# Attention gates and attention branch, four units between the groups of the state-space mixer

## The chip, the cores and the metric

The kernel runs on one core of one Trainium2 chip. The metric is device time of one execution in microseconds (us). TensorE (PE in the rows) multiplies, VectorE (DVE), ScalarE (ACT) and GpSimd (POOL) do elementwise work, and the queue of SyncE (SP) issues most loads from DRAM.

## The reference

A model of two blocks on a sequence of 256 tokens with 1024 features, each block in two layers. The change is in the first block, whose layer reads

```python
u = rms_norm(h, norm_mix[layer])
z, xbc, dt_raw, q, k, v, g_ssd, g_attn = jnp.split(u @ w_in[layer], IN_SPLITS, axis=-1)
y_ssd = ssd_mixer(z, xbc, dt_raw, ...)      # causal conv, SSD in 4 groups of 8 heads, norm per group
y_attn = dilated_attention_mixer(q, k, v, cos, sin)
merged = (jax.nn.sigmoid(g_ssd) * (y_ssd @ w_ssd_branch[layer])
          + jax.nn.sigmoid(g_attn) * (y_attn @ w_attn_branch[layer]))
h = h + merged @ w_out[layer]
u = rms_norm(h, norm_ffn[layer])
h = h + (jax.nn.silu(gate) * up) @ w_down[layer]
```

In `ssd_mixer` the 2048 channels of `x` go through a convolution over 4 tokens and a silu; per group a decay matrix is multiplied into `C B^T` and then with `x * dt`; the result is gated by `silu(z)` and normed over the group's 512 channels. All in float32.

## The kernel before

Every weight matrix is cut into units of 128 x 1024 numbers. `plan()` lists the units in the order of their use, and the weights lie in DRAM in that order, two units to one load of 1 MB (`raw`, three buffers). Each unit is split into a high part `wh` (ScalarE cast, L151) and a low part `wl` = raw - wh (L154, on VectorE or GpSimd), three buffers each, at most `LEAD` = 2 units ahead of the one in use. A product of float32 is then three matmuls: high by high (L465), high by low (L466) and low by high (L467, the one that needs `wl`). A unit of kind "A" has 8 slices of the contraction, so 24 matmuls of 128x256, and adds to a PSUM bank `mm` (three banks); two units (`pairA`) fill a bank.

While `pool_every` = 4 is set (from B and C to the last gate of the state-space mixer), each unit whose number in the plan is divisible by 4 has its low part made by GpSimd (`wl` on POOL), the others by VectorE.

In a layer of the first block come: V, K and Q with attention's two halves, B and C, and then 56 units that concern the change. I number them 0 to 55 in each kernel's own order. Before, they are four groups of eight (four XS units with convolution and silu, four Z units with silu), then eight units of the attention gate (GA), eight of the attention branch, eight of the gate of the state-space mixer (GS). In layer 0 GpSimd's low parts fall on units 0, 4, 8, ..., in layer 1 on units 2, 6, 10, ...; the change leaves this so. After them comes `w_ssd_branch`, in which each output takes two units of 1024 rows: the first reads groups 0 and 1 of the mixer (`yh`, `yl`), the second groups 2 and 3.

Work beside the weights is written as generators. After every unit `tick()` takes one step of each queue: `qa` (attention), `qs` (`ssd_group`) and `qt` (`ssd_tail`). `ssd_group` has six steps: C B^T and its mask `cb` (VectorE, L643), `xdt`, and for each of four pairs of heads the decay `M`: a minimum on VectorE (L659, reads the broadcast `abc`), six exponentials on ScalarE (L668), the product with `cb` on GpSimd (L669), two steps later the matmuls (L678, L679), and then `xs` (L684, L686). The tail squares (`sq`, GpSimd L696 and L697), takes the inverse root (L351, L352), broadcasts it by matmuls (`ch<-c,gr`, L710), scales `xs` (L714) and splits it into `yh` (ScalarE, L359) and `yl` (VectorE, L390).

The order of the program is a wish only: a scheduler lays out each engine's queue before the run, and it may move an instruction ahead of others when its inputs come earlier. On the chip each engine then takes its queue strictly in order. `M` has three buffers, `abc`, `cb` and `xdt` one each; `xs` and `sz` two.

Of the kernel before, what the change touches and what calls it, by code (L numbers as in the profile page):

```python
# [10 lines left out]
F32 = mybir.dt.float32  # L11
F32R = mybir.dt.float32r
BF16 = mybir.dt.bfloat16
AF = mybir.ActivationFunctionType
ALU = mybir.AluOpType
# [3 lines left out]
P = 128  # L19
S = 256  # L20
D = 1024
# [8 lines left out]
C_Z, C_XS, C_B, C_C, C_DT, C_Q, C_K, C_V, C_GS, C_GA = (  # L30
    0, 2048, 4096, 4608, 5120, 5152, 8224, 9248, 10272, 11296)
# [20 lines left out]
def plan():  # L52

    u = []

    def slab(name, layer, k, c0, kind="B", order=None):
        for r in order or range(k // 256):
            u.append((kind, name, layer, 256 * r, c0))  # L60

    def col(name, layer, c0, k=1024):
        for r in range(0, k, 1024):
            u.append(("A", name, layer, r, c0))

    for l in range(DEPTH):
        for n in range(2):
            slab("w_ple_2", l, 256, 512 * n)
    for l in range(DEPTH):
        for half in range(2):  # L70
            slab("w_in", l, D, C_V + 512 * half)
            for c in (C_K, C_Q, C_Q + 1024, C_Q + 2048):
                for f in range(4):
                    col("w_in", l, c + 512 * half + 128 * f)
        for f in range(8):
            col("w_in", l, C_B + 128 * f)
        for g in range(4):
            for f in range(4):
                col("w_in", l, C_XS + 512 * g + 128 * f)
            for f in range(4):  # L80
                col("w_in", l, C_Z + 512 * g + 128 * f)
        for f in range(8):
            col("w_in", l, C_GA + 128 * f)
        for f in range(8):
            col("w_attn_branch", l, 128 * f)
        for f in range(8):
            col("w_in", l, C_GS + 128 * f)
        for f in range(8):
            col("w_ssd_branch", l, 128 * f, 2048)
        for n in range(2):  # L90
            slab("w_out", l, D, 512 * n)
        slab("w_gate_up", l, D, 0, "C")
        for p in range(1, NPAIR):
            for j in (0, 128):
                col("w_gate_up", l, 256 * p + j)
            for j in (0, 128):
                col("w_gate_up", l, FFN + 256 * p + j)
        for n in range(2):
            slab("w_down", l, FFN, 512 * n)
    for l in range(DEPTH):  # L100
        for s in (4, 5, 6):
            slab("w_in_2", l, D, 512 * s)
        for f in range(8):
            col("w_in_2", l, 128 * f)
        for s in (2, 7, 3):
            slab("w_in_2", l, D, 512 * s)
        for n in range(2):
            slab("w_out_2", l, D, 512 * n, order=OUT2_ORDER)
        for n in range(2):
            slab("w_ple_gate_2", l, D, 512 * n)  # L110
    return u


class Weights:


    def __init__(self, tc, nc, dram, raw_pool, hl_pool):
        self.tc = tc
        self.nc, self.dram, self.raw_pool, self.hl_pool = nc, dram, raw_pool, hl_pool
        self.plan = plan()  # L120
        self.end = len(self.plan)
        self.raw = {}
        self.hl = {}
        self.dma_at = self.split_at = self.at = 0
        self.own = {}
        self.first = -9
        self.pool_every = 0
# [130 lines left out]
class Net:  # L258
# [459 lines left out]
    def block1(self, l, h, u, uh, ul):  # L718
        nc = self.nc
# [4 lines left out]
        qa, qs, qt = [], [], []  # L724
# [7 lines left out]
        os = [self.pair([P, 4, S], "O0", "O1")]  # L732
# [9 lines left out]
        for f in range(0, 8, 2):  # L742
            ps = self.pairA("w_in", l, C_B + 128 * f, D, getu)
            self.conv_pair(l, ps, 16 + f, bc[:, f:f + 2, :])
            if f == 0:
                self.drain(qa)
                os.append(self.pair([P, 4, S], "A0", "A1"))
                qa.append(self.attention(*B, *os[1]))
        ytags = ["A2", "A3", "A4", "B0", "B1", "B2", "B3", "B4"]
        ys = []  # L750
        for g in range(4):
            xs = self.sp.tile([P, 4, S], F32, tag="xs", name="xs", bufs=2)
            sz = self.sp.tile([P, 4, S], F32, tag="sz", name="sz", bufs=2)
            for f in (0, 2):
                ps = self.pairA("w_in", l, C_XS + 512 * g + 128 * f, D, getu)
                self.conv_pair(l, ps, 4 * g + f, xs[:, f:f + 2, :])
            for f in (0, 2):
                ps = self.pairA("w_in", l, C_Z + 512 * g + 128 * f, D, getu)
# [4 lines left out]
            yh, yl = self.pair([P, 4, S], ytags[2 * g], ytags[2 * g + 1])  # L763
            ys.append((yh, yl))
            qs.append(self.ssd_group(l, g, bc, xs, sz, dts, yh, yl, qt))

        def halves(tiles):
            return [tiles[f // 4][:, f % 4:f % 4 + 2, :] for f in range(0, 8, 2)]

        ga = halves([self.sp.tile([P, 4, S], F32, tag="u", name="ga", bufs=2) for _ in range(2)])  # L770
        for f in range(0, 8, 2):
            ps = self.pairA("w_in", l, C_GA + 128 * f, D, getu)
            nc.scalar.activation(ga[f // 2], ps, AF.Tanh, scale=0.5)
        self.drain(qa)
        for f in range(0, 8, 2):
            ps = self.pairA("w_attn_branch", l, 128 * f, D, lambda k: (*os[k // 4], k % 4))
            nc.vector.scalar_tensor_tensor(ga[f // 2], ga[f // 2], 1.0, ps, ALU.add, ALU.mult)
        gs = self.sp.tile([P, KD, S], F32, tag="big", name="gs")
        for f in range(0, 8, 2):
            ps = self.pairA("w_in", l, C_GS + 128 * f, D, getu)  # L780
# [4 lines left out]
        for f in range(0, 8, 2):  # L785
# [3 lines left out]
            ps = self.pairA("w_ssd_branch", l, 128 * f, 2 * D, lambda k: (*ys[k // 4], k % 4))  # L789
# [30 lines left out]
        for p in range(1, NPAIR):  # L820
# [10 lines left out]
            f = 2 * (p % 2)  # L831
# [372 lines left out]
def _layout(x):  # L1204
    w = np.empty((len(plan()), P, 1024), np.float32)
    for n, (kind, name, l, r, c) in enumerate(plan()):
        k, width = (8, 128) if kind == "A" else (2, 512)
        m = x[name][l, r:r + k * P]
        if kind == "A" and name == "w_in" and C_Q <= c < C_V:
            m = m[:, c + ROPE1]  # L1210
            c = 0
        m = m[:, c:c + width] if kind != "C" else np.concatenate([m[:, c:c + 256], m[:, FFN + c:FFN + c + 256]], axis=1)
        w[n] = m.reshape(k, P, width).transpose(1, 0, 2).reshape(P, 1024)
    w = np.ascontiguousarray(w.reshape(-1, 2, P, 1024).transpose(0, 2, 1, 3)).reshape(-1, P, 2048)
    wdt = x["w_in"][:, :, C_DT:C_DT + 32].reshape(DEPTH, 8, P, 32).transpose(2, 0, 1, 3).reshape(P, DEPTH, 256)
    conv = np.concatenate([x["conv_w"], x["conv_b"][:, None, :]], axis=1)
    conv = conv.reshape(DEPTH, 5, 24, P).transpose(3, 0, 2, 1).reshape(P, DEPTH, 120)
    dsk = np.repeat(x["d_skip"], 64, axis=1).reshape(DEPTH, 16, P).transpose(2, 0, 1)
    sn = x["ssd_norm"].reshape(DEPTH, 16, P).transpose(2, 0, 1)
    feat = np.concatenate([conv, dsk, sn], axis=2)  # L1220
    rows = np.stack([x["dt_bias"][0], x["a_log"][0], x["dt_bias"][1], x["a_log"][1]])
    i, j = _positions()
    bias2 = np.take(x["rel_bias_2"], _bucket(np.maximum(i - j, 0)), axis=0).transpose(0, 2, 1)
    pT = x["p_2"][:, 0].transpose(0, 2, 1).reshape(DEPTH, 2, P, S).transpose(0, 2, 1, 3)
    c1, c2 = _consts()
    out = dict(w=w, wdt=wdt, feat=feat, rows=rows, bias2=bias2, pT=pT, consts=c1, consts2=c2, x=x["x"][0])
    for n in ("norm_mix", "norm_ffn", "norm_final", "norm_g_2", "ret_norm_g_2", "q_norm_g_2", "k_norm_g_2",
              "ple_norm_g_2"):
        out[n] = x[n]
    return {n: np.ascontiguousarray(v) for n, v in out.items()}  # L1230
# [19 lines left out]
```

## Time and profile before

| | |
|---|---|
| median of 3 runs | 1624.92 us (1623.88 to 1625.94) |
| the profiled execution | 1624.88 us |
| its span of instructions | 1623.1 us |
| TensorE busy in the span | 1569.8 us |
| VectorE, ScalarE, GpSimd busy | 1126.9, 800.7, 485.2 us |
| data from HBM | 278.69 MB, mean 174 GB/s |

The profiled execution's time is its span and 1.8 us around it. In layer 0 the 56 units run from about 180 to 384 us of the span, in layer 1 from about 810 to 1025 us. A matmul counts as busy until its modelled end, so TensorE's busy share says little on its speed; its idle time and the number of instructions in a stretch (the figure behind x) say more.

### The profile page before, as it was taken

To read this page: it belongs to the slowest core of one execution; us is meant where nothing else is said; L and a number is where in the kernel's file an instruction comes from. 1 tells how busy PE (TensorE), PEld (TensorE's weight loads), DVE (VectorE), ACT (ScalarE), POOL (GpSimd) and SP (SyncE) were. 2 spreads that over 40 slices of the span, in tenths; PEclk is the share of its full clock that TensorE was granted. 3 is DMA by queue.
4 is the path that set the end of the run, shared out by engine and by line. 5 is a ranking of instruction groups with operands and counts; after the bars stand their busy time and mean duration, and the time that the engine had idled before them with its cause. 6 is when DMAs were issued, how large, how long until landed. Compare 5 with 4: busy or idle time off the path is not lost.

```text
span 1623.1 us, 26819 instructions
## 1 busy us (share of the span) xinstructions
PE 1569.8 (97%) x10904; PEld 1443.0 (89%) x10904; DVE 1126.9 (69%) x1634; ACT 800.7 (49%) x1256; POOL 485.2 (30%) x298
## 2 busy tenths in 40 slices
PE   9999999999999999999999889999999899989998
PEld 6999989899989987899998889988998679868986
DVE  5768998964665655677899865465565667666765
ACT  5444667544434444344476654443443445454543
POOL 3546257731020001245445753010000252141212
PEclk9999999999999999999999999999999999999999
DMA  8544534465545555454444445554555555454542
GB/s 348 172 167 143 191 136 156 165 215 183 182 168 183 182 184 205 156 180 158 150 164 134 178 141 202 185 205 143 183 184 193 192 190 188 144 181 147 185 149 104
DMA packets 43373, 284.67 MB, mean 175 GB/s; under 512 B 4817, under 2 KB 6225, under 8 KB 10866
## 3 DMA queue, kind: packets, MB, share of 16 engines
q1 hardware_dynamic: 41314, 271.37, 48.5%
q0 software_dynamic: 1936, 11.60, 1.8%
q8 instruction: 85, 1.39, 0.3%
q14 instruction: 38, 0.31, 0.1%
HBM read 278.69 MB, written 4.26 MB: 174 GB/s over the span
## 4 chain that ended last, share of the span: by engine, by line
PE 84%; DVE 7%; POOL 3%; ACT 3%; issue 2%; DMA 1%; SPq 0%; POOLq 0%; ACTq 0%; DVEq 0%
PE mm L465 17%; PE mm L467 17%; PE mm L466 17%; PE mm L402 8%; PE mm L403 8%; PE mm L404 8%; PE tr L366 2%; DVE u L210 2%; DVE wl L154 2%; DMA raw<-in_w_dram 1%; PE ch L523 1%; POOL wfirst L154 1%; ACT wh L151 1%; PE ch L678 1%; ACT wfirst L151 1%
## 5 line engine op out<-in xcount | busy, mean ns | idle before, releaser
L154 DVE TENSOR_TENSOR wl<-raw,wh 128x1024 fp32r<-128x1024 f32 x422 | 573.7, 1364 | 310.5 <-ACT wh L151 308.9
L151 ACT CAST wh<-raw 128x1024 fp32r<-128x1024 f32 x454 | 474.3, 1048 | 560.2 <-PE mm L466 395.5
L467 PE MATMUL mm<-uh,wl 128*128 128x256 f32 x2176 | 617.9, 284 | 9.3 <-DVE wl L154 5.9
L465 PE MATMUL mm<-uh,wh 128*128 128x256 f32 x2176 | 620.5, 285 | 1.6 <-ACT wh L151 1.1
L466 PE MATMUL mm<-ul,wh 128*128 128x256 f32 x2176 | 616.2, 283 | 0.0
L467 PEld LDWEIGHTS mm<-uh,wl 128*128 128x128 f32 x2176 | 411.6, 189 | 11.5 <-DVE wl L154 6.6
L465 PEld LDWEIGHTS mm<-uh,wh 128*128 128x128 f32 x2176 | 411.8, 189 | 6.3 <-issue 4.2
L466 PEld LDWEIGHTS mm<-ul,wh 128*128 128x128 f32 x2176 | 411.4, 189 | 1.3 <-issue 0.9
L154 POOL TENSOR_TENSOR wfirst<-raw,wfirst 128x1024 fp32r<-128x1024 f32 x24 | 62.0, 2594 | 550.9 <-ACT wfirst L151 550.7
L154 POOL TENSOR_TENSOR wl<-raw,wh 128x1024 fp32r<-128x1024 f32 x32 | 77.2, 2412 | 108.7 <-ACT wh L151 98.8
L403 PE MATMUL mm<-wl,uh 128*128 128x512 f32 (+1 forms) x220 | 87.2, 396 | 0.4 <-DVE wl L154 0.3
L404 PE MATMUL mm<-wh,ul 128*128 128x512 f32 (+1 forms) x220 | 86.2, 392 | 0.0
L402 PE MATMUL mm<-wh,uh 128*128 128x512 f32 (+1 forms) x220 | 86.0, 400 | 0.0
L485 POOL TENSOR_TENSOR qT<-qT,rot 64x512 f32<-64x512 f32 x32 | 57.4, 1794 | 92.8 <-ACT qT L481 92.8
L669 POOL TENSOR_TENSOR M<-M,cb 128x768 f32<-128x768 f32 x32 | 67.9, 2138 | 12.9 <-DVE cb L643 6.5
L629 DVE SCALAR_TENSOR_TENSOR acc<-mm,feat,acc 128x255 f32<-128x255 f32 (+2 forms) x144 | 67.2, 475 | 5.2 <-ACT acc L627 4.1
L402 PE MATMUL mm<-wfirst,uh 128*128 128x512 f32 (+1 forms) x140 | 58.3, 416 | 2.2 <-ACT uh L382 1.2
L403 PE MATMUL mm<-wfirst,uh 128*128 128x512 f32 (+1 forms) x140 | 57.4, 410 | 0.3 <-DVE wfirst L154 0.3
L404 PE MATMUL mm<-wfirst,ul 128*128 128x512 f32 (+1 forms) x140 | 56.6, 404 | 0.0
L486 POOL TENSOR_TENSOR qT<-qT,rp 64x512 f32<-64x512 f32 x32 | 49.8, 1555 | 20.7 <-DVE rp L483 20.7
L465 PE MATMUL mm<-A,wh 128*128 128x256 f32 x192 | 54.0, 281 | 0.0
L466 PE MATMUL mm<-B,wh 128*128 128x256 f32 x192 | 54.0, 281 | 0.0
(298 smaller groups left out, 2695.9 us busy)
## 6 DMA issues: line engine op xcount, KB each, us to landing
raw<-in_w_dram SPq DMA_DIRECT2D x243, 1024.0 KB, 4.8
abc<-scr POOLq DMA_DIRECT2D x8, 1024.0 KB, 6.1
es<-e POOLq DMA_DIRECT2D x4, 512.0 KB, 11.4
e<-es SPq DMA_DIRECT2D x4, 512.0 KB, 5.0
raw<-in_w_dram SPq DMA_DIRECT2D x2, 512.0 KB, 5.0
h<-in_x_dram SPq DMA_DIRECT2D x2, 512.0 KB, 8.9
h<-in_x_dram SPq DMA_DIRECT2D x1, 1024.0 KB, 5.7
gain<-in_norm_ffn_dram SPq DMA_DIRECT2D x2, 512.0 KB, 5.3
```

The source lines that it names most:

```text
L151: self.nc.scalar.copy(h, raw)
L154: eng.tensor_tensor(lo, raw, h.bitcast(F32), ALU.subtract)
L402: nc.tensor.matmul(ps, xh[:, k0 + k, ts], hw[:, k, :], start=start and k == 0, stop=False)
L403: nc.tensor.matmul(ps, xh[:, k0 + k, ts], lw[:, k, :], start=False, stop=False)
L404: nc.tensor.matmul(ps, xl[:, k0 + k, ts], hw[:, k, :], start=False, stop=stop and k == 1)
L465: nc.tensor.matmul(ps, hw[:, k, :], xh[:, kx, :], start=j == 0 and k == 0, stop=False)
L466: nc.tensor.matmul(ps, hw[:, k, :], xl[:, kx, :], start=False, stop=False)
L467: nc.tensor.matmul(ps, lw[:, k, :], xh[:, kx, :], start=False, stop=j == n - 1 and k == 7)
L485: nc.gpsimd.tensor_tensor(dst[0:64], dst[0:64], self.cc1[0:64, None, :].to_broadcast([64, 2, S]), ALU.mult)
L486: nc.gpsimd.tensor_tensor(dst[0:64], dst[0:64], b[0:64], ALU.add)
L629: nc.vector.scalar_tensor_tensor(acc[:, j, k:S], ps[:, j, 0:S - k], w[:, 3 - k:4 - k], acc[:, j, k:S], ALU.mult, ALU.add)
L669: nc.gpsimd.tensor_tensor(m, m, cb[:, None, :].to_broadcast([P, 2, 384]), ALU.mult)
```

## The change

The list of units and the body of `block1` change in the same way. After group 0 and after group 1 come four units of the attention gate each, after group 2 and after group 3 four units of the attention branch each. GS follows as before. So the 56 units are now: group 0 in 0 to 7, gate 8 to 11, group 1 in 12 to 19, gate 20 to 23, group 2 in 24 to 31, branch 32 to 35, group 3 in 36 to 43, branch 44 to 47, GS 48 to 55. The number of instructions stays, `drain(qa)` ahead of the branch goes (the one in group 1 remains), and the tiles of the gate are taken ahead of the loop. The line numbers of the changed kernel are one higher in the helpers and 14 higher in the Z part of the loop.

```diff
@@ plan()
-        for f in range(8):
-            col("w_in", l, C_GA + 128 * f)
-        for f in range(8):
-            col("w_attn_branch", l, 128 * f)
+            for f in range(4 * (g % 2), 4 * (g % 2) + 4):
+                if g < 2:
+                    col("w_in", l, C_GA + 128 * f)
+                else:
+                    col("w_attn_branch", l, 128 * f)
@@ block1()
+        ga = halves([self.sp.tile([P, 4, S], F32, tag="u", name="ga", bufs=2) for _ in range(2)])
+
+        def gate(f):
+            ps = self.pairA("w_in", l, C_GA + 128 * f, D, getu)
+            nc.scalar.activation(ga[f // 2], ps, AF.Tanh, scale=0.5)
+
+        def branch(f):
+            ps = self.pairA("w_attn_branch", l, 128 * f, D, lambda k: (*os[k // 4], k % 4))
+            nc.vector.scalar_tensor_tensor(ga[f // 2], ga[f // 2], 1.0, ps, ALU.add, ALU.mult)
+
         for g in range(4):
...
             qs.append(self.ssd_group(l, g, bc, xs, sz, dts, yh, yl, qt))
-        ga = halves([self.sp.tile([P, 4, S], F32, tag="u", name="ga", bufs=2) for _ in range(2)])
-        for f in range(0, 8, 2):
-            ps = self.pairA("w_in", l, C_GA + 128 * f, D, getu)
-            nc.scalar.activation(ga[f // 2], ps, AF.Tanh, scale=0.5)
-        self.drain(qa)
-        for f in range(0, 8, 2):
-            ps = self.pairA("w_attn_branch", l, 128 * f, D, lambda k: (*os[k // 4], k % 4))
-            nc.vector.scalar_tensor_tensor(ga[f // 2], ga[f // 2], 1.0, ps, ALU.add, ALU.mult)
+            for f in (4 * (g % 2), 4 * (g % 2) + 2):
+                (gate if g < 2 else branch)(f)
```

Three places show what moved. First VectorE in layer 1 while group 0 is worked off beside the last head of attention (`acc`, `xs<-xs,acc`: convolution and silu; `M`, `xs<-xs,feat,ch`: `ssd_group`; `E,m`: attention). Before:

```order
L154 TENSOR_TENSOR wl<-raw,wh 128x1024
L629 SCALAR_TENSOR_TENSOR acc<-mm,feat,acc 128x255
L629 SCALAR_TENSOR_TENSOR acc<-mm,feat,acc 128x254
L629 SCALAR_TENSOR_TENSOR acc<-mm,feat,acc 128x253
L659 TENSOR_TENSOR M<-abc,d_acum 128x2x2x128
L154 TENSOR_TENSOR wl<-raw,wh 128x1024
L659 TENSOR_TENSOR M<-abc,d_acum 128x2x2x128
L629 SCALAR_TENSOR_TENSOR acc<-mm,feat,acc 128x255
L629 SCALAR_TENSOR_TENSOR acc<-mm,feat,acc 128x254
L629 SCALAR_TENSOR_TENSOR acc<-mm,feat,acc 128x253
L684 SCALAR_TENSOR_TENSOR xs<-xs,feat,ch 128x256 x2
L629 SCALAR_TENSOR_TENSOR acc<-mm,feat,acc 128x255
```

and now:

```order
L155 TENSOR_TENSOR wl<-raw,wh 128x1024
L660 TENSOR_TENSOR M<-abc,d_acum 128x2x2x128
L155 TENSOR_TENSOR wl<-raw,wh 128x1024
L660 TENSOR_TENSOR M<-abc,d_acum 128x2x2x128
L685 SCALAR_TENSOR_TENSOR xs<-xs,feat,ch 128x256 x2
L526 ISA E,m_9115<-ch,mask_a 128x256
L526 ISA m_9115 128x1
L528 ISA E,m_9115<-ch,mask_a 128x128
L528 ISA m_9115 128x1
```

The convolution of group 1 no longer stands among these rows; it comes later in the queue.

Second GpSimd's queue in layer 0 from the tail of group 0 over the start of `ssd_group` 1 (`E`: attention, `M`: decay, `sq` and `gr`: tail, `abc`: broadcast of the next group). Before:

```order
L686 TENSOR_TENSOR xs<-xs,sz 128x512
L541 TENSOR_TENSOR E<-E 128x384
L696 TENSOR_TENSOR sq<-sq 128x512
L669 TENSOR_TENSOR M<-M,cb 128x768 x2
L697 TENSOR_TENSOR sq<-sq 128x256
L669 TENSOR_TENSOR M<-M,cb 128x768
L154 TENSOR_TENSOR wl<-raw,wh 128x1024
L352 TENSOR_TENSOR gr<-rs_v,nhalf 128x2
```

and now:

```order
L687 TENSOR_TENSOR xs<-xs,sz 128x512
L542 TENSOR_TENSOR E<-E 128x384
L697 TENSOR_TENSOR sq<-sq 128x512
L698 TENSOR_TENSOR sq<-sq 128x256
L353 TENSOR_TENSOR gr<-rs_v,nhalf 128x2
L155 TENSOR_TENSOR wl<-raw,wh 128x1024
L670 TENSOR_TENSOR M<-M,cb 128x768 x3
L155 TENSOR_TENSOR wl<-raw,wh 128x1024
L639 DMA abc<-scr 128x2048
```

The squares of the tail stand ahead of the three products `M` and no longer among them, and a low part `wl` now stands directly behind the three.

Third VectorE in layer 1 at the end of the 56 units (`rs_v`, `xs<-xs,feat,ch`, `B`: tail of group 3; `ga`, `gs`: gates). Before:

```order
L351 TENSOR_SCALAR rs_v<-ch 128x2
L154 TENSOR_TENSOR wl<-raw,wh 128x1024 x2
L777 SCALAR_TENSOR_TENSOR ga<-ga,mm 128x512
L714 SCALAR_TENSOR_TENSOR xs<-xs,feat,ch 128x256 x4
L390 TENSOR_TENSOR B_10009<-xs,B_10008 128x1024
L154 TENSOR_TENSOR wl<-raw,wh 128x1024
L777 SCALAR_TENSOR_TENSOR ga<-ga,mm 128x512
L154 TENSOR_TENSOR wl<-raw,wh 128x1024 x2
L777 SCALAR_TENSOR_TENSOR ga<-ga,mm 128x512
L154 TENSOR_TENSOR wl<-raw,wh 128x1024 x10
L791 SCALAR_TENSOR_TENSOR gs<-gs,mm 128x512
```

and now:

```order
L685 SCALAR_TENSOR_TENSOR xs<-xs,feat,ch 128x256 x2
L155 TENSOR_TENSOR wl<-raw,wh 128x1024 x3
L352 TENSOR_SCALAR rs_v<-ch 128x2
L155 TENSOR_TENSOR wl<-raw,wh 128x1024 x2
L715 SCALAR_TENSOR_TENSOR xs<-xs,feat,ch 128x256 x4
L155 TENSOR_TENSOR wl<-raw,wh 128x1024
L391 TENSOR_TENSOR B_10387<-xs,B_10386 128x1024
L155 TENSOR_TENSOR wl<-raw,wh 128x1024 x3
L795 SCALAR_TENSOR_TENSOR gs<-gs,mm 128x512
```

The scaling and the split of the last group's `xs` have moved behind the low parts of GS, to directly ahead of `gs`, which belongs to `w_ssd_branch`.

## Rows read from the trace of the kernel before

**Rows 1.** Busy time by engine, whole span: us, share, instructions.
```profile
PE 1569.8 (97%) x10904; PEld 1443.0 (89%) x10904; DVE 1126.9 (69%) x1634; ACT 800.7 (49%) x1256; POOL 485.2 (30%) x298
```

**Rows 2.** Stretches of 20 us: busy us by engine, granted clock, DMA.
```profile
220.00:240.00 20.00, 17.82 (x143) 15.83 (x142) 19.02 (x38) 10.66 (x23) 10.40 (x7) 1.00 0.45 151
240.00:260.00 20.00, 19.11 (x151) 17.81 (x151) 16.69 (x23) 15.75 (x35) 16.57 (x11) 1.00 0.34 113
...
280.00:300.00 20.00, 19.69 (x163) 17.57 (x161) 19.96 (x26) 10.31 (x18) 16.22 (x10) 1.00 0.54 200
300.00:320.00 20.00, 18.95 (x158) 18.43 (x155) 19.12 (x21) 15.11 (x31) 14.57 (x7) 1.00 0.38 125
320.00:340.00 20.00, 19.68 (x166) 18.07 (x166) 15.53 (x17) 10.91 (x18) 12.47 (x9) 1.00 0.63 218
...
400.00:420.00 20.00, 20.00 (x171) 20.00 (x170) 11.52 (x13) 8.60 (x9) 0.00 (x0) 1.00 0.56 184
...
860.00:880.00 20.00, 16.28 (x135) 15.32 (x134) 19.93 (x34) 12.25 (x26) 10.96 (x8) 1.00 0.32 108
...
900.00:920.00 20.00, 15.56 (x122) 14.52 (x119) 19.66 (x22) 13.33 (x28) 15.15 (x7) 0.96 0.31 107
...
940.00:960.00 20.00, 14.76 (x106) 14.27 (x105) 13.42 (x11) 8.52 (x16) 12.06 (x6) 0.83 0.32 106
```

**Rows 3.** Stretches of 5 us in layer 1, same columns.
```profile
920.00:925.00 5.00, 5.00 (x38) 4.68 (x37) 3.08 (x8) 1.95 (x4) 1.39 (x2) 0.80 0.57 203
955.00:960.00 5.00, 4.74 (x24) 4.74 (x25) 0.20 (x1) 0.06 (x1) 0.79 (x1) 0.55 0.62 210
960.00:965.00 5.00, 5.00 (x45) 4.57 (x44) 1.99 (x3) 2.90 (x5) 1.55 (x2) 1.00 0.35 100
```

**Rows 4.** Waits of PE, layer 1, 840 to 960 us: total, times, longest.
```profile
PE mm L467 <- DVE wl L154: 4.9, 1, 4.9
PE mm L467 <- POOL wl L154: 2.9, 1, 2.9
PE tr L366 <- DVE E L543: 2.0, 1, 2.0
```

**Rows 5.** Waits of PE, layer 0, 200 to 345 us, same columns.
```profile
PE tr L366 <- DVE E L543: 2.2, 1, 2.2
```

**Rows 6.** DVE in order of time: start, duration, instruction, idle before it.
```profile
308.79 0.55 DVE L643 TENSOR_TENSOR cb<-ch,c 128x384 f32<-128x384 f32 x1
...
936.69 0.68 DVE L632 SCALAR_TENSOR_TENSOR xs<-xs,acc 128x512 f32<-128x512 f32 x1
...
951.83 3.38 DVE L154 TENSOR_TENSOR wl<-raw,wh 128x1024 fp32r<-128x1024 f32 x1
961.02 1.23 DVE L154 TENSOR_TENSOR wl<-raw,wh 128x1024 fp32r<-128x1024 f32 x1 [5.81 <-ACT wh L151]
...
991.38 1.65 DVE L714 SCALAR_TENSOR_TENSOR xs<-xs,feat,ch 128x256 f32<-128x256 f32 x4
```

**Rows 7.** POOL in order of time, layer 0, then layer 1.
```profile
309.51 6.87 POOL L669 TENSOR_TENSOR M<-M,cb 128x768 f32<-128x768 f32 x3 [2.73 <-DVE cb L643]
316.35 2.27 POOL L696 TENSOR_TENSOR sq<-sq 128x512 f32<-128x512 f32 x1
318.58 2.39 POOL L154 TENSOR_TENSOR wl<-raw,wh 128x1024 fp32r<-128x1024 f32 x1
...
951.79 2.33 POOL L154 TENSOR_TENSOR wl<-raw,wh 128x1024 fp32r<-128x1024 f32 x1
```

**Rows 8.** PE in order of time, layer 0, then layer 1.
```profile
305.94 0.59 PE L640 MATMUL ch<-bc 128*128 128x256 f32 x2
...
309.43 0.60 PE L366 MATMUL tr<-c,xs 128*128 128x128 f32 x4
...
990.58 0.61 PE L710 MATMUL ch<-c,gr 128*128 128x128 f32 x4
```

**Rows 9.** ACT in order of time, layer 1.
```profile
993.07 1.05 ACT L359 CAST B<-xs 128x1024 fp32r<-128x1024 f32 x1 [1.35 <-DVE xs L714]
```

More of the change, by code (lines that the diff above doesn't have):

```diff
@@ L748, in block1, with halves @@
                 qa.append(self.attention(*B, *os[1]))
+        def halves(tiles):
+            return [tiles[f // 4][:, f % 4:f % 4 + 2, :] for f in range(0, 8, 2)]
+        ga = halves([self.sp.tile([P, 4, S], F32, tag="u", name="ga", bufs=2) for _ in range(2)])
[5 more added lines that the diff above has]
+            nc.vector.scalar_tensor_tensor(ga[f // 2], ga[f // 2], 1.0, ps, ALU.add, ALU.mult)
         ytags = ["A2", "A3", "A4", "B0", "B1", "B2", "B3", "B4"]
@@ L765, in block1 @@
             qs.append(self.ssd_group(l, g, bc, xs, sz, dts, yh, yl, qt))
-        def halves(tiles):
-            return [tiles[f // 4][:, f % 4:f % 4 + 2, :] for f in range(0, 8, 2)]
-        ga = halves([self.sp.tile([P, 4, S], F32, tag="u", name="ga", bufs=2) for _ in range(2)])
-        for f in range(0, 8, 2):
-            ps = self.pairA("w_in", l, C_GA + 128 * f, D, getu)
-            nc.scalar.activation(ga[f // 2], ps, AF.Tanh, scale=0.5)
-        self.drain(qa)
-        for f in range(0, 8, 2):
-            ps = self.pairA("w_attn_branch", l, 128 * f, D, lambda k: (*os[k // 4], k % 4))
-            nc.vector.scalar_tensor_tensor(ga[f // 2], ga[f // 2], 1.0, ps, ALU.add, ALU.mult)
+            for f in (4 * (g % 2), 4 * (g % 2) + 2):
+                (gate if g < 2 else branch)(f)
         gs = self.sp.tile([P, KD, S], F32, tag="big", name="gs")
```

## The prediction

> **What bounds the kernel now.** I read the busy times first: TensorE is busy for 1569.8 us of a span of 1623.1 us [rows 1], so an order that changes no work can win only from the 53 us in which it is idle and from stretches in which its clock falls. Next I cut the span into stretches of 20 us and looked for those in which TensorE is short of 20.00. In the 56 units of layer 0 it is short by 2.18 us in 220 to 240, 0.89 in 240 to 260, 0.31, 1.05 and 0.32 in the three from 280 to 340: 4.75 us [rows 2]. In layer 1 it is 3.72 us in 860 to 880, 4.44 in 900 to 920 and 5.24 in 940 to 960: 13.4 us [rows 2]. The reader is to see VectorE in the same rows: 19.02, 19.96, 19.12, 19.93 and 19.66 of 20 us where TensorE starves, against 11.52 us in 400 to 420, where nothing but units and their low parts run and TensorE does 171 instructions without a gap [rows 2]. So work of VectorE is heaped on the groups, and the gate and branch units behind them have slack.
>
> The idle time in layer 1 also costs clock. In 920 to 925 and 955 to 960 the granted clock is 0.80 and 0.55, each behind a wait, and TensorE does 38 and 24 instructions where a stretch at 1.00 holds 45 [rows 3]. That is 7/45 of 5 us = 0.8 us, and 4.74 us less 24/9 us = 2.0 us: 2.8 us. All that the groups lose is thus 4.75 + 13.4 + 2.8 = 21.0 us.
>
> Third, the waits by name. The two longest in layer 1 are for low parts `wl`, 4.9 us for one of VectorE and 2.9 us for one of GpSimd [rows 4]; after them, in both layers, TensorE's transpose waits for attention's `E`, 2.0 and 2.2 us [rows 4, 5]. The queues show why low parts come late. A VectorE low part takes 1.23 us alone (at 961.02) and 3.38 us beside a low part of GpSimd that began 0.04 us before it and took 2.33 us [rows 6, 7]; so what GpSimd does delays VectorE as well. And GpSimd works its three products `M` in one go once `cb` is there, 6.87 us, then `sq` 2.27 us, then `wl` 2.39 us: the low part is done 11.5 us after the burst began [rows 7].
>
> The Trainium skill states this as a rule (SBUF — State Buffer, "Who interferes with whom"): a VectorE instruction with two SBUF inputs and a GpSimd instruction that reads SBUF cannot run at once, and the later one waits out the other. By that rule the low part at 951.83 should take 2.33 + 1.23 = 3.56 us, and the row has 3.38, so the trace agrees.
>
> **What the change does, part by part.** Nothing is added or removed: the same units, low parts, loads and steps. What moves are 16 units a layer, at 24 matmuls each. TensorE's 171 instructions in 20 us [rows 2] make 2.8 us for a unit, so each group gets four units, 11.2 us, in which VectorE has little but low parts. A group's own work runs in the six ticks after it, so four of its six steps now fall into those units.
>
> Gain, layer 0. The wait for `E` of 2.2 us stands in the first ticks behind group 0, where TensorE's queue and GpSimd's are as before; I keep it. The others, 4.75 - 2.2 = 2.6 us, go. Layer 1: the same kind of wait, 2.0 us, I keep, since `E` is behind GpSimd work there too; the other 11.4 us go, and with them the 2.8 us of clock, since no wait of 3 us or more is left. Sum of the gain: 2.6 + 11.4 + 2.8 = 16.8 us. Its bounds: 21.0 us if the waits for `E` go too, and nothing if the waits only move.
>
> Cost, the low part behind the burst. In layer 0 GpSimd's queue has a `wl` directly behind the three `M` of groups 1, 2 and 3, and TensorE wants it at units 24, 36 and 48. I count from the broadcast of the tail, which comes about when the unit four places earlier starts. VectorE and GpSimd: broadcast 0.61 [rows 8], scaling 1.65, a low part 1.23, the silus of Z and XS 0.68 each, the tail's low part 1.23 (the form of a `wl`), `cb` 0.55 [rows 6], then the three `M` 6.87 and `wl` 2.39 [rows 7]: 15.9 us. TensorE: broadcast 0.61, four units 11.2, C B^T 0.59, two sets of transposes at 0.60 [rows 8], and about as much again for the first products of the pairs: 14.2 us. So it waits 1.7 us, three times: 5.1 us. The bounds are 0 (VectorE takes some of these rows before the broadcast) and 4.0 us each (`M` and `wl` as far apart as before, with 2.27 us between them).
>
> In layer 1 the low part behind the burst follows only after the next broadcast's load, the fourth `M` and an `xs`, and is wanted two units later. The same sequence stood there before, five units behind `cb`, and TensorE's waits have only one for a GpSimd low part, 2.9 us, which came behind a burst and `sq` [rows 4]. So each of the three costs between 0 and 2.9 us; the nearest row is the sequence that cost nothing, and I take 0.5 us each: 1.5 us.
>
> Cost, the last tail. It had 12 units of cover and now ends with GS. Its chain is 0.61 + 1.65 + 1.05 for the cast [rows 6, 8, 9] and 1.23 for the low part, 4.5 us; one low part of a unit stands between scaling and split on VectorE, mostly beside the cast: 4.7 us. `w_ssd_branch` needs group 3 in the middle of its second unit, 0.61 + 1.5 x 2.8 = 4.8 us on. I take 0.2 us a layer, 0.4 us; if a cast and a low part get ahead it is 1.05 + 1.23 = 2.3 us a layer.
>
> What costs nothing: the tiles of the gate are taken earlier, from buffers that the norm's `u` left before; the load of `h` for the residual goes out five loads later on SP's queue, behind the last use of `abc`, and its reader comes only with `w_out`, 16 units on. Were that cover gone, the loads of two or three units would stand behind it. PSUM banks for the new units are those of the old ones.
>
> Sum: 16.8 - 5.1 - 1.5 - 0.4 = 9.8 us less. The profiled execution took 1624.88 us, its span and 1.8 us; the median is 1624.92. So 1624.9 - 9.8 = **1615.1 us**.
>
> **Rivals.** (1) All waits go: if VectorE has slack in every stretch, `cb` and `E` come early too. 1624.9 - 21.0 = 1603.9 us. For it speaks the load: VectorE had 19 to 20 of 20 us busy and gets a third more time for each group. Against it: both waits for `E` sit beside GpSimd's work, which stays.
>
> (2) The waits move with the bursts. GpSimd's seconds are the same, each group still has its burst behind `cb`, and VectorE's low parts beside it take 3.38 instead of 1.23 us. If each burst holds TensorE for 2.5 to 3 us, six of them give back 15 to 18 us of the 16.8: 1623 to 1626 us. For it: both long waits of layer 1 lie beside such bursts. Against it: `sq` has left the burst, and VectorE has less queued behind it. The skill's rule above is this rival's: issue order, not load, decides who waits, so thinner load on VectorE would not help.
>
> (3) Slower: the low part behind the burst, in both layers. If `cb` is as late as the rows add up and the burst runs with the 2.27 us more that it had, TensorE waits 4.0 us at units 24, 36 and 48 of layer 0 and 26, 38 and 50 of layer 1: 24 us, against a gain of 16.8. 1624.9 - 16.8 + 24 = 1632 us. It decides from 2.8 us a wait on. Against it: layer 1 has two units, 5.6 us, more than layer 0.
>
> (4) The last tail is late: 2.3 us twice on top of the forecast instead of 0.4: 1615.1 + 4.2 = 1619.3 us.
>
> **How the numbers follow.** Forecast 0.46 (its own range 1609 to 1620), rival 1 0.16, rival 2 0.19, rival 3 0.10, rival 4 0.09. About 0.2% or 3.2 us is what a measurement of this kernel can tell from no change. Faster is then the forecast, rivals 1 and 4 and a little of 2: 0.73. The same is most of rival 2: 0.17. Slower is rival 3: 0.10. The range from 1605 to 1622 us leaves out most of rivals 2 and 3 above and the fastest end of rival 1 below; its ends take in 0 to 2.5 us for each wait of layer 0.
>
> **What would show it.** Right: in layer 1 VectorE's busy time in the stretches from 860 to 960 falls below 19 us, the waits of 4.9 and 2.9 us are gone, no stretch there has a clock under 0.9, and both layers take about equally long for the 56 units; small waits for a `wl` of GpSimd appear at units 24, 36 and 48 of layer 0. Rival 2 would show six waits of 2.5 us beside `M`, rival 3 waits of 4 us, rival 4 a wait of TensorE in the second unit of `w_ssd_branch`. Wrong altogether would be a wait at a place that none of these names.

## The result, and the profile after

The changed kernel takes 1606.65 us (median of 4 runs, 1604.33 to 1611.75) against 1625.43 us for the kernel before on the same chip (4 runs, 1623.88 to 1626.95): a ratio of 0.9889, 95% interval 0.9863 to 0.9915. It is faster by 18.8 us (by the interval 14 to 22), where 9.8 were forecast. Its profiled execution took 1607.53 us, 1605.7 of them the span.

First the page's busy times [rows 1]:

```profile
PE 1567.0 (98%) x10904; PEld 1440.6 (90%) x10904; DVE 1118.2 (70%) x1634; ACT 801.5 (50%) x1256; POOL 490.2 (31%) x298
```

TensorE's work is the same 10904 matmuls; its idle time in the span fell from 53.3 to 38.7 us. To see where, I cut out the 56 units of each layer, from the first matmul of unit 0 to that of the unit behind unit 55 (columns: stretch, its length, busy us of PE, PEld, DVE, ACT and POOL, granted clock, DMA share, GB/s). Before, layer 0 and layer 1:

```profile
179.80:383.50 203.70, 198.94 (x1627) 189.47 (x1626) 164.87 (x262) 124.49 (x226) 109.78 (x63) 1.00 0.51 175
810.00:1025.20 215.20, 201.63 (x1618) 191.51 (x1617) 166.50 (x250) 124.21 (x225) 109.16 (x61) 0.98 0.48 167
```

After:

```profile
177.70:383.20 205.50, 201.74 (x1627) 191.24 (x1625) 164.92 (x258) 124.61 (x226) 113.91 (x63) 0.99 0.50 173
809.80:1007.60 197.80, 196.96 (x1619) 188.12 (x1617) 152.50 (x245) 123.35 (x225) 109.88 (x61) 1.00 0.52 182
```

Layer 1 gained 17.4 us, 12.7 of it TensorE's idle time (13.57 to 0.84); layer 0 lost 1.8. Layer 0 began 2.1 us earlier; 17.4 - 1.8 + 2.1 is the span's 17.4 within 0.3. Those 2.1 us come from the start of the kernel, which the change leaves alone. From 20 to 40 us, before and after:

```profile
20.00:40.00 20.00, 18.09 (x87) 14.63 (x86) 8.63 (x12) 8.77 (x15) 9.67 (x8) 0.91 0.94 389
20.00:40.00 20.00, 18.95 (x104) 15.79 (x104) 9.56 (x13) 9.94 (x16) 9.67 (x8) 1.00 0.95 393
```

The profile before has 0.9 us more of waits of TensorE there, a granted clock of 0.91 and 17 matmuls fewer. The new order with place 2 (below) has 0.91 and 87 matmuls there too, so this is not the order's doing. The part that the two profiles show of the order itself is 17.4 - 1.8 = 15.6 us.

The stretches of 20 us that answer to [rows 2], one of layer 0 and three of layer 1, and one stretch of 5 us in layer 0:

```profile
220.00:240.00 20.00, 19.13 (x140) 17.39 (x141) 13.65 (x27) 11.16 (x27) 10.19 (x7) 0.91 0.44 158
...
860.00:880.00 20.00, 20.00 (x171) 19.41 (x169) 18.24 (x33) 16.43 (x36) 9.23 (x7) 1.00 0.37 113
...
900.00:920.00 20.00, 19.16 (x161) 18.10 (x160) 14.00 (x19) 14.20 (x30) 12.91 (x8) 1.00 0.52 189
...
940.00:960.00 20.00, 20.00 (x168) 18.60 (x167) 13.33 (x23) 15.29 (x33) 12.98 (x9) 1.00 0.54 186
...
220.00:225.00 5.00, 4.13 (x20) 3.61 (x21) 3.65 (x5) 2.34 (x7) 0.64 (x1) 0.70 0.43 123
```

In layer 1 the clock is 1.00 and TensorE is full but for the 0.84 us in 900 to 920, which is the wait for `sq` below. VectorE goes from 19.93, 19.66 and 13.42 us to 18.24, 14.00 and 13.33: in the stretch in which TensorE had lost most, 940 to 960, its load is as it was. In layer 0 the granted clock is 0.70 of 2.4 GHz in the stretch that holds a wait, so TensorE ran a part of it at 1.2 GHz.

TensorE's waits (total, times, longest; one of 0.2 us left out) in layer 0 from 175 to 400 us [rows 5]:

```profile
PE tr L367 <- DVE E L544: 2.2, 1, 2.2
PE ch L703 <- POOL sq L698: 1.0, 1, 1.0
PE mm L468 <- POOL wl L155: 0.2, 1, 0.2
```

and the only one in layer 1, from 790 to 1060 us [rows 4]:

```profile
PE ch L703 <- POOL sq L698: 0.8, 1, 0.8
```

The waits of 4.9 and 2.9 us for low parts are gone, and so is layer 1's wait for `E`. GpSimd's queue shows what changed (start, duration, instruction, idle before it). Layer 1 before, ahead of the low part at 951.79 of [rows 7]:

```profile
943.73 5.90 POOL L669 TENSOR_TENSOR M<-M,cb 128x768 f32<-128x768 f32 x3 [3.81 <-DVE cb L643]
949.59 2.24 POOL L696 TENSOR_TENSOR sq<-sq 128x512 f32<-128x512 f32 x1
```

Layer 1 after, group 1:

```profile
884.49 2.40 POOL L155 TENSOR_TENSOR wl<-raw,wh 128x1024 fp32r<-128x1024 f32 x1 [2.53 <-ACT wh L152]
888.33 8.29 POOL L670 TENSOR_TENSOR M<-M,cb 128x768 f32<-128x768 f32 x3 [1.44 <-DVE cb L644]
...
902.79 2.38 POOL L155 TENSOR_TENSOR wl<-raw,wh 128x1024 fp32r<-128x1024 f32 x1
```

Before, the low part stood behind the three `M` and half of `sq`, and the low part of VectorE for which TensorE waited 4.9 us ran beside it (951.83, 3.38 us). Now one is made ahead of the burst and the next only 6 us after its end. The order of the units did not change which units GpSimd serves; it changed what stands in front of them.

### The profile page after: what moved, and what is told of

Same layout as the page of the kernel before. It is cut to its first block, busy times and chain, and to the rows that moved or that the text cites. A ratio compares the mean times of both kernels' runs of the same rounds, so it can differ in the third digit from the quotient of the medians.

```text
span 1605.7 us, 26834 instructions
## 1 busy us (share of the span) xinstructions
PE 1567.0 (98%) x10904; PEld 1440.6 (90%) x10904; DVE 1118.2 (70%) x1634; ACT 801.5 (50%) x1256; POOL 490.2 (31%) x298
## 4 chain that ended last, share of the span: by engine, by line
PE 89%; DVE 3%; POOL 3%; ACT 2%; DMA 2%; issue 1%; SPq 0%; POOLq 0%; ACTq 0%; DVEq 0%
PE mm L466 19%; PE mm L468 18%; PE mm L467 18%; PE mm L403 8%; PE mm L404 8%; PE mm L405 8%; PE tr L367 2%; DVE u L211 2%; PE ch L524 1%; DMA raw<-in_w_dram 1%; PE ch L679 1%; POOL wfirst L155 1%; ACT wh L152 1%; ACT wfirst L152 1%; PE ch L525 1%
## 5 line engine op out<-in xcount | busy, mean ns | idle before, releaser
L155 DVE TENSOR_TENSOR wl<-raw,wh 128x1024 fp32r<-128x1024 f32 x422 | 566.7, 1348 | 290.6 <-ACT wh L152 288.9
L670 POOL TENSOR_TENSOR M<-M,cb 128x768 f32<-128x768 f32 x32 | 72.0, 2266 | 34.4 <-DVE cb L644 26.7
L468 PE MATMUL mm<-A,wl 128*128 128x256 f32 x192 | 54.1, 282 | 0.0
```

The source lines that it names most:

```text
L155: eng.tensor_tensor(lo, raw, h.bitcast(F32), ALU.subtract)
L468: nc.tensor.matmul(ps, lw[:, k, :], xh[:, kx, :], start=False, stop=j == n - 1 and k == 7)
L670: nc.gpsimd.tensor_tensor(m, m, cb[:, None, :].to_broadcast([P, 2, 384]), ALU.mult)
```

## The experiments

I held three explanations against each other. One: the new order gives VectorE room, so any layer should gain. Two: the gain is the loss of the bad meeting of GpSimd's low part with the burst of `M` and `sq`, and depends on which units are GpSimd's. Three: a low part on GpSimd is itself the harm, by what it costs VectorE.

"Place p" is the remainder by 4 of a unit's number (0 to 55) at which GpSimd makes the low part. The kernel before, and the one after, have place 0 in layer 0 and place 2 in layer 1. As every group is 8 units long before and 12 after, both multiples of 4, a place falls on the same spot of every group.

**The change in one layer alone.**

```diff
+SPREAD = (1,)
...
+            if l not in SPREAD:
+                continue
...
```

`(1,)` is layer 1 alone, `(0,)` layer 0 alone; a layer that is not named takes its gate and branch units behind the four groups, as before.

> The new order in layer 1 alone; layer 0 in the old order. Theory A (the time came from the waits and the slow clock of layer 1 alone, 17.4 us by the starts of its units in the two profiles): 17 to 18 us less than before, 1607 to 1609 us. Rival B (what counts is the third more time that each group gives VectorE, the same in both layers): about half of the gain, 1616 us.

Measured: 1607.66 us, ratio 0.9893 (0.9879 to 0.9908), as the whole change. Layer 1 took 198.2 us, layer 0 205.1.

> The new order in layer 0 alone; layer 1 in the old order. Theory A: 0 to 2 us either way, 1623 to 1627 us, and layer 1 keeps its waits of 3 to 5 us for a low part. Rival B: about half of the gain, 1616 us.

Measured: 1624.69 us, ratio 1.0002 (0.9990 to 1.0013). Layer 0 took 204.3 us, and layer 1, in the old order, 218.0, with waits of 5.8 and 3.0 us for low parts. So the gain is layer 1's alone; explanation one, that any layer gains, falls.

**The place alone.** The next kernels set the place by

```diff
-            pool = ... or self.pool_every and i % self.pool_every == 0
+            pool = ... or self.pool_every and i % self.pool_every == self.phase
...
+        self.w.phase = 2 * l
```

in the old order (`before`) or the new one (`after`). The same place is set in both layers: `2 * l` is place 0, `2 - 2 * l` place 2, `(1 + 2 * l) % 4` place 1, `(3 + 2 * l) % 4` place 3.

> The kernel before, with GpSimd's low parts of layer 1 on units 0, 4, 8, ... as in layer 0 in place of 2, 6, 10, .... Theory C (layer 1 was slow because its GpSimd low parts stand behind a burst of M and sq, which the place in four decides): layer 1 becomes like layer 0, 203.7 in place of 215.2 us for the 56 units, so 11 us less, 1614 us, without any new order. Rival D (the load on VectorE decides, whichever unit GpSimd takes): within 3 us of before.

Measured: 1614.09 us, ratio 0.9933 (0.9917 to 0.9950); layers 206.3 and 206.0. Some 10 us are to be had with no unit moved.

> The old order, GpSimd's low parts on units 2, 6, 10, ... in both layers. Theory (place 2 under the old order is what made layer 1 slow, and layer 0 is slow by as much when it is put there): both layers 215 to 218 us, 11 to 14 us slower than before, 1636 to 1639 us. Rival (layer 1's loss has a cause of its own, other than the place): within 3 us of before.

Measured: 1635.5 us, ratio 1.0062 (1.0046 to 1.0079); layers 215.7 and 215.3. Layer 0 now has layer 1's waits (175 to 400 us): first the three longest of TensorE, then GpSimd around the one of 4.8 us, which ends at 324.19 with a low part of VectorE that started 0.04 us behind GpSimd's (at 320.75) and took 3.38 us:

```profile
PE mm L467 <- DVE wl L154: 4.8, 1, 4.8
PE mm L467 <- POOL wl L154: 3.0, 1, 3.0
PE tr L366 <- DVE E L543: 2.0, 1, 2.0
...
312.66 5.89 POOL L669 TENSOR_TENSOR M<-M,cb 128x768 f32<-128x768 f32 x3 [3.81 <-DVE cb L643]
318.51 2.25 POOL L696 TENSOR_TENSOR sq<-sq 128x512 f32<-128x512 f32 x1
320.71 2.34 POOL L154 TENSOR_TENSOR wl<-raw,wh 128x1024 fp32r<-128x1024 f32 x1
```

Layer 1's loss before was its place, not the layer.

> The changed kernel, with GpSimd's low parts of layer 0 on units 2, 6, 10, ... as in layer 1. Theory C: layer 0 becomes like layer 1, 198 in place of 203 to 205 us for the 56 units, since no low part stands directly behind the three M and beside attention's E: 4 to 7 us less than the changed kernel, 1600 to 1603 us. Rival D: the place makes no difference once the order is spread, within 2 us of the changed kernel.

Measured: 1601.11 us (1599.81 to 1602.56), ratio 0.9853 (0.9837 to 0.9870), the fastest of all, ahead of both kernels. Layers 197.6 and 199.7, TensorE idle for 0.7 and 1.4 us:

```profile
180.80:378.30 197.50, 196.84 (x1617) 188.06 (x1616) 151.66 (x246) 123.77 (x226) 111.13 (x61) 1.00 0.51 179
803.60:1003.40 199.80, 198.40 (x1619) 189.59 (x1617) 152.61 (x245) 123.30 (x225) 109.80 (x61) 0.99 0.52 180
```

> The new order in both layers, GpSimd's low parts on units 0, 4, 8, ... in both. Theory (what counts is where a low part falls against the bursts of M and sq and against attention's E; at place 0 the new order wins nothing over the old one): both layers 204 to 206 us, 1611 to 1615 us. Rival (the new order has a gain of its own in layer 1 whatever the place): layer 1 at 197 to 200 us, 1606 to 1609 us.

Measured: 1613.81 us, ratio 0.9930 (0.9915 to 0.9944); layers 204.4 and 205.8. At place 0 the new order is worth nothing over the old (1614.09).

Where place 0 loses in the new order can be read at the wait for `E`. The kernel after in layer 0, GpSimd and then VectorE (`E<-E,mx` is the normalising step that TensorE waits for):

```profile
215.03 1.47 POOL L542 TENSOR_TENSOR E<-E 128x384 f32<-128x384 f32 x1
216.46 2.38 POOL L155 TENSOR_TENSOR wl<-raw,wh 128x1024 fp32r<-128x1024 f32 x1
218.79 1.85 POOL L670 TENSOR_TENSOR M<-M,cb 128x768 f32<-128x768 f32 x1
...
216.53 2.45 DVE L543 TENSOR_SCALAR E<-E,mx 128x256 f32<-128x256 f32 x1 [0.31 <-POOL E L542]
218.91 1.82 DVE L544 TENSOR_SCALAR E<-E,mx 128x128 f32<-128x128 f32 x1
```

and with place 2 (new order):

```profile
215.26 2.00 POOL L542 TENSOR_TENSOR E<-E 128x384 f32<-128x384 f32 x1
217.22 1.84 POOL L670 TENSOR_TENSOR M<-M,cb 128x768 f32<-128x768 f32 x1
...
217.51 1.69 DVE L543 TENSOR_SCALAR E<-E,mx 128x256 f32<-128x256 f32 x1
219.13 0.28 DVE L544 TENSOR_SCALAR E<-E,mx 128x128 f32<-128x128 f32 x1
```

The 128x128 step takes 0.28 us by itself and 1.82 us when it starts 0.12 us behind an `M`; the 128x256 step ends 0.14 us after the low part that it started behind. From the end of `E<-E` on GpSimd to the ready `E` it takes 4.2 us with the low part there (216.50 to 220.73) and 2.2 without (217.26 to 219.41), and no wait for `E` is left. By the Trainium skill (SBUF — State Buffer, Who interferes with whom) a tensor-scalar of VectorE can enter a mode that takes the port pair shared with GpSimd, and then the one issued later waits out the whole other instruction. Both rows agree: VectorE's instruction ends 0.14 and 0.09 us behind GpSimd's. The idle time accounts for about half of the 6.9 us by which layer 0 is shorter at place 2 (4.1 us idle at place 0, 0.7 at place 2). The rest stands inside TensorE's busy time and is not traced.

> The kernel before, with GpSimd's low parts of both layers on units 1, 5, 9, .... Theory C, sharpened: what counts is how far behind the burst of M the next GpSimd low part is wanted; on units 2 of 4 it is two units, on 0 of 4 four. On 1 of 4 it is wanted one unit behind or, if the scheduler puts it ahead of the burst, five. Ahead of the burst: both layers at about 200 us, 1605 to 1611 us; behind it: both layers lose as layer 1 did, 1632 to 1640 us. Rival D (load on VectorE, 0 of 4 was luck): 1620 to 1627 us.

Measured: 1630.53 us, ratio 1.0041 (1.0026 to 1.0055); both layers 212. In groups 1 to 3 of layer 0 the low part stood ahead of the burst (from 246.26, 281.19 and 313.90 us), in group 0 between its products (219.25). The 1605 to 1611 us expected of "ahead" were missed: the kernel was slower than before. Its three longest waits in layer 0:

```profile
PE tr L366 <- DVE E L543: 6.1, 2, 3.9
PE ch L702 <- POOL sq L697: 2.3, 1, 2.3
PE mm L467 <- DVE wl L154: 1.7, 1, 1.7
```

The waits for GpSimd's low part are gone, and those for attention's `E` and the tail's `sq` took their place. The longest, 3.9 us, stands in group 0, but the other 2.2 us for `E`, the 1.7 and the 2.3 us stand beside the bursts of groups 1 and 3. So "ahead of the burst" is not enough.

> The new order, GpSimd's low parts on units 1, 5, 9, ... in both layers. In GpSimd's queue the low parts of units 33 and 45 then stand behind the burst of three M of their own unit. Theory (the place against the burst decides): waits of 4 to 5 us at two units of each layer, 1615 to 1625 us. Rival (the new order is robust against the place): 1600 to 1606 us.

Measured: 1631.4 us, ratio 1.0035 (1.0016 to 1.0053), above the range expected; its 10 runs spread from 1620.05 to 1634.41, and the profiled one, with layers of 213.1 and 217.6 us, was the slowest. A low part stands behind the burst and the next between the two halves of `sq`:

```profile
265.22 7.31 POOL L670 TENSOR_TENSOR M<-M,cb 128x768 f32<-128x768 f32 x3 [5.52 <-DVE cb L644]
272.47 2.84 POOL L155 TENSOR_TENSOR wl<-raw,wh 128x1024 fp32r<-128x1024 f32 x1
...
288.96 1.29 POOL L697 TENSOR_TENSOR sq<-sq 128x512 f32<-128x512 f32 x1 [3.90 <-ACT sq L696]
290.20 2.38 POOL L155 TENSOR_TENSOR wl<-raw,wh 128x1024 fp32r<-128x1024 f32 x1
292.54 1.71 POOL L698 TENSOR_TENSOR sq<-sq 128x256 f32<-128x256 f32 x1
```

and TensorE waits less for low parts than for other results, of which `gr` comes behind the half of `sq` that a low part delays (that the others are late for the same reason is not shown):

```profile
PE tr L367 <- DVE E L544: 3.9, 1, 3.9
PE ch L711 <- POOL gr L353: 2.7, 1, 2.7
PE mm L466 <- DVE acc L630: 1.9, 1, 1.9
PE mm L468 <- POOL wl L155: 1.0, 1, 1.0
```

I had expected waits for `wl` of 4 to 5 us; the place decides, but by other waits than I named. The granted clock of both layers is 0.97, against 1.00 and 0.99 at place 2, so the waits cost more than their own length.

> The new order, GpSimd's low parts on units 3, 7, 11, ... in both layers. The low part stands ahead of the burst of M, as at place 2. Theory (the place against the burst decides): 1600 to 1606 us, layers of 197 to 200 us. Rival (attention's E is pushed back instead, as with the old order at place 1): waits for E of 2 us or more, 1608 to 1614 us.

Measured: 1611.03 us, ratio 0.9910 (0.9893 to 0.9928); layers 203.1 and 203.9. The theory's 1600 to 1606 us were missed. The time is the rival's, but not its wait for `E` of 2 us or more: the waits are small and many (`sq` 1.6, `xs` 1.2, `E` 0.8 us in layer 0).

**No low parts on GpSimd in the 56 units.**

```diff
-POOL_EVERY = 4
+POOL_EVERY = 0
```

> The kernel before with all low parts of the 56 units on VectorE, none on GpSimd: 16 more a layer at 1.2 us. Theory C (GpSimd's late low parts hold TensorE, not VectorE's load): about as with units 0 of 4 or better, 1608 to 1616 us. Rival D: VectorE, 19 to 20 of 20 us busy in the groups, gets 10 us more work in the four groups of each layer, and the old order loses 10 to 20 us: 1635 to 1645 us.

Measured, old order: 1611.6 us, ratio 0.9924 (0.9905 to 0.9943); layers 204.4 and 203.6.

> The changed kernel with all low parts of the 56 units on VectorE. If the new order gives VectorE the room, as the prediction said (about 18 of 20 us busy now, and 1.2 us more for every fourth unit, 11 us), it holds within 3 us of the changed kernel with units 2 of 4 in both layers: 1599 to 1605 us. If VectorE's room was not needed for the gain but is not there either: 1608 to 1615 us.

Measured, new order: 1612.36 us, ratio 0.9929 (0.9902 to 0.9957); layers 207.3 and 206.7 in the profiled run, which was the slowest of four (1616.79). Expected were 1599 to 1605: missed. Without GpSimd's low parts the new order gains nothing either. Explanation three is half right: the old order, at the places it had, is better off without GpSimd's help (by 13 us), the new order at place 2 is better off with it (by 11 us). Layer 0 of the old order:

```profile
180.00:384.40 204.40, 200.81 (x1626) 190.20 (x1626) 172.09 (x277) 123.80 (x226) 80.78 (x49) 1.00 0.49 173
```

**The squares of the tail on VectorE** (old order).

```diff
-        nc.gpsimd.tensor_tensor(sq[:, 0:2, :], sq[:, 0:2, :], sq[:, 2:4, :], ALU.add)
-        nc.gpsimd.tensor_tensor(sq[:, 0, :], sq[:, 0, :], sq[:, 1, :], ALU.add)
+        nc.vector.tensor_tensor(sq[:, 0:2, :], sq[:, 0:2, :], sq[:, 2:4, :], ALU.add)
+        nc.vector.tensor_tensor(sq[:, 0, :], sq[:, 0, :], sq[:, 1, :], ALU.add)
```

> The kernel before with the two sums sq of each tail (2.0 and 1.4 us on GpSimd) on VectorE, so that a low part of GpSimd comes 2.3 to 4 us sooner behind the burst, and VectorE gets four groups of two sums more a layer. Theory C: layer 1's waits of 2.9 and 4.9 us shrink by 2 us or more each and the slow clock behind them goes: 1616 to 1620 us. Rival D: VectorE's load grows by 6 us or more a layer and so does the time: 1628 to 1636 us.

Measured: 1631.57 us, ratio 1.0049 (1.0032 to 1.0065); layers 213.4 and 217.4. Rival D's time came, not theory C's 1616 to 1620 us. The waits for low parts went, and waits for VectorE's `xdt` (up to 3.0 us), `xs` and `sq` came. Taking two instructions out of the burst is no cure when the engine that gets them is the one with 19 of 20 us busy.

All orders and places together, medians in us (the kernel before ran at 1624.45 to 1625.43 beside them):

| GpSimd's low parts | old order | new order |
|---|---|---|
| place 0 in both layers | 1614.09 | 1613.81 |
| place 1 | 1630.53 | 1631.4 |
| place 2 | 1635.5 | 1601.11 |
| place 3 | not run | 1611.03 |
| none | 1611.6 | 1612.36 |
| 0 in layer 0, 2 in layer 1 | 1625.43 | 1606.65 |

The order is worth 34 us at place 2, and less than 1 us at places 0, 1 and none, which is within what these runs can tell from no change. The last row is a layer of each: 17 us from the layer at place 2, nothing from the one at place 0. Neither explanation one nor three can give this table. Of explanation two the second half is shown: time depends on which units are GpSimd's. Its first half, that the harm is the meeting with the burst of `M` and `sq`, is borne out at place 2 in either order; at places 1 and 3 it gave the wrong forecast. What remains open is a rule that says beforehand which place is good: "ahead of the burst" holds for place 2 in the new order and fails for place 1 in the old. By the waits at places 0 and 1 such a rule would have to count all that GpSimd's low part delays, `sq`, `gr` and VectorE's steps on `E` too; no run tests one.

## Why the prediction was right, and where not

**What bounds the kernel.** Right: TensorE's waits in layer 1's groups were the prize, and layer 1 gave all of the gain. VectorE's busy time is below 19 us in each of the stretches, as forecast, but that was a companion and not the cause: in 940 to 960, where TensorE lost most (5.24 us), VectorE had only 13.42 us before, a figure that the prediction's list of VectorE's loads leaves out. "Each group gets four units in which VectorE has little" is true of all places, and at places 0, 1 and none it brought nothing. So the mechanism, room on VectorE, was wrong as stated: with layer 1's low parts at place 0 as well, the same order takes 1613.81 us against 1614.09. That layer 1 had place 2, where the order gains, is luck, and the time came within the range by 1.7 us at its lower end.

**Gain, layer 1.** The step kept 2.0 us for `E` and took 11.4 + 2.8. The `E` wait went as well, and the low parts behind the burst cost nothing against 1.5 us. Forecast net 12.5 us with the last tail's 0.2, measured 17.4. Of that, 12.7 us are idle time and 4.7 are busy time. The low clock was some 3.3 us of the latter, not 2.8, by the matmuls behind the two waits: 13 intervals in 2.93 us and 19 in 4.22, where one takes 0.12 at full clock. The 0.8 us of the first left out what ran before 920 us. The other 1.4 us are not traced.

**Gain, layer 0.** 2.6 us were forecast to go; idle time fell only from 4.8 to 3.8 us. The 2.2 us for `E` stayed, as said; so did a wait for `sq` (0.9 us before, 1.0 after, from GpSimd), which the prediction names nowhere and counted among those that go. In the profiled run the wait for `E` also cost clock, for which the prediction had no term: it gave only longer waits a price in clock. The new order with place 0 has the same layer 0 and the same wait at a granted clock of 1.00:

```profile
220.00:225.00 5.00, 4.07 (x29) 3.49 (x30) 3.72 (x5) 2.32 (x8) 0.70 (x1) 1.00 0.37 111
```

From the end of the wait to the next product of attention (`ch<-pT,v`) the kernel after took 5.14 us (220.87 to 226.01) and this one 3.62 (220.93 to 224.55): 1.5 us of clock. The layer's loss was 1.8 us in the profile against 2.7 forecast, near in sum by luck: idle time fell by 1.0 where 2.6 were forecast, the low parts behind the bursts cost 0.2 where 5.1 were, and TensorE's busy time grew by 2.8 us, 1.5 of it clock and 1.3 not traced.

**Cost, the low part behind the burst.** The mis-sized term: 5.1 us in layer 0, measured 0.2. The sequence is there, on GpSimd in group 1:

```profile
262.91 6.35 POOL L670 TENSOR_TENSOR M<-M,cb 128x768 f32<-128x768 f32 x3 [7.06 <-DVE cb L644]
269.19 3.38 POOL L155 TENSOR_TENSOR wl<-raw,wh 128x1024 fp32r<-128x1024 f32 x1
```

and on TensorE from the broadcast to the first use of that low part:

```profile
256.23 0.60 PE L711 MATMUL ch<-c,gr 128*128 128x128 f32 x4
...
272.31 0.39 PE L466 MATMUL mm<-uh,wh 128*128 128x256 f32 x1
...
272.74 0.66 PE L679 MATMUL ch<-M,xdt 128*64 128x256 f32 x4
273.22 0.40 PE L680 MATMUL ch<-M,xdt 128*64 128x128 f32 x4
273.55 0.38 PE L468 MATMUL mm<-uh,wl 128*128 128x256 f32 x1
```

VectorE's and GpSimd's side was well counted: the low part is done 16.3 us after the broadcast, against 15.9. TensorE's side was not: it comes to unit 24 after 16.1 us and to the product that needs the low part after 17.3, where I had 14.2. I left out most of the products of the pairs, which the burst itself releases: two sets of four stand behind the high product of unit 24 and cover the rest. The lower bound, 0, was the true one.

**Cost, the last tail.** The 16 units of `w_ssd_branch` took 45.57 us before and 45.66 after in both layers, from their first matmul to the first of `w_out`: 0.1 us against 0.2 a layer.

**The sum and the rivals.** 16.8 - 7.0 was forecast and 18.8 measured (17.4 in the profiles); the time lies 8.5 us below the forecast and 2.7 above rival 1, in which all waits go. For layer 1 that rival was the better account. For layer 0 it was wrong: its reason, slack of VectorE in every stretch, should have freed that layer too. Rival 2, that the waits move with the bursts, comes out at places 0 and 1 as far as the gain goes, which is nil there, though by other waits than it named. Its condition, that the order of the queue and not VectorE's load decides, was nearer the truth than mine; layer 1's place happens to suit the new order. Rivals 3 and 4 did not occur. The waits for `sq` of 1.0 and 0.8 us stand at a place that none of the prediction's signs names; they are small, but in layer 1 they are all that is left. "Both layers take about equally long" was wrong: 205.5 and 197.8 us.

The step that I lacked was to ask, for each layer by itself, which instruction of GpSimd stands ahead of each of its low parts in either order. I did so for the cost, and took the gain from VectorE's load.

## What to carry to other kernels

When work is handed out by a counter (every fourth unit) and the rest of the kernel repeats with a multiple of that period, each piece meets much the same neighbours in every repetition, for good or ill. Before judging an order, run it at each phase of the counter: here order and phase together decided between 1601 and 1636 us, and the order alone was worth nothing at two of the three phases that were run in both. An engine that takes its queue in order is judged by what stands ahead of the piece that somebody waits for, not by its busy share.

## What the runs showed of the hardware

Taking 14 instructions (29.0 us) off GpSimd in layer 0 of the old order and giving VectorE 15 more raised VectorE's busy time by 7.2 us (164.87 to 172.09), while 15 low parts of 1.23 us alone [rows 6] are 18.5. So each low part that GpSimd made had cost VectorE some 0.75 us in longer instructions, an estimate from one pair of profiles: the offload saved VectorE two fifths of the low parts' own time and not all of it.

The same wait of 2.2 us for `E`, at the same place of layer 0, was followed by a granted clock of 0.70 in the profile after and by 1.00 in that before [rows 2, 5]; the new order with place 0, whose layer 0 is that of the kernel after, has 1.00 too. So a single wait of this size may or may not cost clock (here 1.5 us) with the same queue, and a term for it has both ends.
